# Output projections turned round (512 tokens move past stationary weights), the second norm's row factor moved into what follows it, and x reordered by loads

## The chip, the cores and the metric

One Trainium2 chip, one of its cores. Five engines work side by side, each through its own list of instructions in order: TensorE (PE; its weight loads are listed as PEld), VectorE (DVE), ScalarE (ACT), GpSimd (POOL), and SyncE (SP), which here issues all DMAs. The metric is the time of one execution in microseconds, as the median of several runs; lower is better.

## The reference

Two layers over 1024 tokens and 1024 model columns, all float32:

```python
def reference(x, positions, norm_g, fox_w_in, ..., dsw_w_out):
    cos, sin = rotary_tables(positions)
    for i in range(DEPTH):                      # DEPTH = 2
        h = rms_norm(x, norm_g[i])
        if i % N_MIXERS == 0:                   # layer 1: forgetting attention, 16 heads of 64, causal
            o, gate = fox_mixer(h, fox_w_in[j], fox_b_f[j], fox_q_norm[j], fox_k_norm[j])
            w_out = fox_w_out[j]
        else:                                   # layer 2: 3 groups of dilated windows, dilations 1, 4, 16
            o, gate = dsw_mixer(h, cos, sin, dsw_w_in[j], dsw_q_norm[j], dsw_k_norm[j])
            w_out = dsw_w_out[j]
        x = x + (o * jax.nn.silu(gate)) @ w_out
    return x

def rms_norm(x, g):
    y = x * lax.rsqrt(jnp.mean(x * x, axis=-1, keepdims=True) + EPS) * g
```

The part that matters here is the end of each layer: the mixer's output times the gate, called y below, goes through a 1024 x 1024 output projection and is added to x; between the layers the sum is normed by rows (tokens) and becomes the input of layer 2. Layer 2 norms its queries and keys per head of 64, so that a factor on a whole token's row cancels there but for EPS; values and gates carry it.

## The kernel before, in words

**Operands.** TensorE takes the left operand by columns: `xh[p, k, s]` holds row k*128+p of the transposed activations for token s, rounded to float32r, and `xl` what the rounding left. Weights are split the same way into `w.slabs[k][:, 0]` (high) and `[:, 1]` (low): ACT rounds a slab (L286), POOL or DVE subtracts (L288). A product is three matmuls: xh with high, xh with low, xl with high. `project` (L305) makes one tile of 128 tokens: for each of 8 k it loads 128 x 128 of xh or xl as the stationary operand and moves up to 384 weight columns past it. The result `pj` lies with tokens on partitions.

**Stages, in order.** (1) Gate columns of layer 1 in three parts of 384, 256 and 384 columns (`PARTS`), written to DRAM as `gs_d`. (2) Eight pairs of heads: project q, k, v of a pair for 8 token tiles, with the attention of these tiles spread among the projections (`fox_tile`: scores in PSUM tile `s`, DVE's min pass L659, ACT's exp L493, split into two halves `ph`, a DMA transpose into `ptt` L500, products with the values into `o`). Outputs y go to DRAM `y_d`; for the last pair they stay. (3) Output projection of layer 1, three parts by 8 token tiles. (4) Gates of layer 2. (5) 24 steps of dilated attention. (6) Output projection of layer 2.

**The order of the work.** PE's order is written out: `Flow` counts ticks (one for each two k of a projection, four for a token tile, 32 for a part), and work is queued for a tick (`flow.at`). `due` and `lsd` in `CFG` say at which ticks attention comes. The other engines and SP's list of DMAs are ordered by a list scheduler from that; each engine, and SP too, then runs its list strictly in order, so that a waiting instruction holds up those behind it.

**Turning y.** y has tokens on partitions and must be turned before a projection. `turn_y` loads seven of eight column blocks of a token tile back from `y_d` and turns them on PE (`transpose_rows`, L324), then ACT copies to xh (L327) and DVE makes xl (L328). The eighth block, of the last pair of heads, comes by `turn_last`. In stage 3, `project(..., t)` for a tile t needs the y of this tile alone.

**Between the layers.** In the third part of stage 3, each token tile's finished row of the sum, `xf`, is collected (two thirds of it loaded back from `x1_d`), normed on the spot (`norm_rows`: sums of squares on ACT, factor, product with the gain row `gbc` on DVE), written to `xn_d`, and turned by eight PE transposes into xh and xl for stage 4 (L785). In the eighth step of stage 5, `reload_x` (L917) loads the same rows from `xn_d` in another token order (every fourth token) and turns them on PE once more.

**Pools.** PSUM tiles: `pj` in a pool of three, scores `s` in three, `o` in two. x and sums for stage 3 pass through `n2k`, three buffers.

## Time and profile before

| what | value |
|---|---|
| time, median of 3 runs (lowest to highest) | 1817.96 us (1817.16 to 1822.23) |
| time of the profiled execution | 1825.77 us |
| its span, in which the trace lies | 1824.0 us |
| PE busy in the span | 1756.8 us (96%) |
| DVE, ACT, POOL busy | 1110.7, 985.2, 950.9 us |
| mean granted clock of TensorE | 0.992 |
| stage 3 (first to last of its additions) | 538.2 to 672.0 us |
| stage 4 (first to last of its gate inputs, L475) | 678.2 to 766.1 us |
| stage 6 (first to last of its additions) | 1727.9 to 1821.1 us |

The stages' ends are read from the first and last start of the lines L777, L780, L475 and L979. A group's row in the profile says how long instructions of a kind ran and how long their engine had stood idle before them; the timeline puts that idle time in brackets, with what ended it. A window's row says how much of a stretch each engine was busy; the rest of PE's stretch is its idle time.

### The profile page before, as it was taken

To read this page: it belongs to the slowest core of one execution; us is meant where nothing else is said; L and a number is where in the kernel's file an instruction comes from. 1 tells how busy PE (TensorE), PEld (TensorE's weight loads), DVE (VectorE), ACT (ScalarE), POOL (GpSimd) and SP (SyncE) were. 2 spreads that over 40 slices of the span, in tenths; PEclk is the share of its full clock that TensorE was granted. 3 is DMA by queue.
4 is the path that set the end of the run, shared out by engine and by line. 5 is a ranking of instruction groups with operands and counts; after the bars stand their busy time and mean duration, and the time that the engine had idled before them with its cause. 6 is when DMAs were issued, how large, how long until landed. Compare 5 with 4: busy or idle time off the path is not lost.

```text
span 1824.0 us, 39234 instructions
## 1 busy us (share of the span) xinstructions
PE 1756.8 (96%) x13784; PEld 1691.7 (93%) x13784; DVE 1110.7 (61%) x3774; ACT 985.2 (54%) x2642; POOL 950.9 (52%) x1161
## 2 busy tenths in 40 slices
PE   7999999999979989999999999999999999999999
PEld 6999888888868989999999999999999999999899
DVE  8546666766665373365556665676676766767631
ACT  6536666666664354445555565555555555555610
POOL 3215666556653211255556555667576666757520
PEclk9999999999999999999999999999999999999999
DMA  8347999899998563356676786676776766667852
GB/s 286 114 119 139 183 202 187 174 178 185 200 201 186 166 205 112 114 114 140 125 142 138 157 193 133 146 154 145 145 152 153 166 148 139 154 143 176 196 140 93
DMA packets 630790, 289.28 MB, mean 159 GB/s; under 512 B 510384, under 2 KB 595376, under 8 KB 630592
## 3 DMA queue, kind: packets, MB, share of 16 engines
q1 hardware_dynamic: 630592, 286.77, 69.1%
q8 instruction: 108, 1.77, 0.4%
q14 instruction: 90, 0.74, 0.1%
HBM read 124.87 MB, written 37.03 MB: 89 GB/s over the span
## 4 chain that ended last, share of the span: by engine, by line
PE 45%; DMA 21%; DVE 10%; ACT 8%; POOL 7%; issue 7%; SPq 1%; DVEq 0%; POOLq 0%; ACTq 0%
PE pj L312 40%; DMA raw<-in_w_dsw 6%; DMA ptt<-ph 4%; DMA raw<-in_w_fox 3%; POOL w L288 3%; PE s L448 2%; POOL ph L499 2%; DMA qk_t<-hl 2%; DVE p L659 2%; ACT p L493 2%; ACT ph L496 1%; POOL hl L423 1%; DMA raw<-in_w_fgate 1%; DMA x_d<-xo 1%; DVE u L420 1%
## 5 line engine op out<-in xcount | busy, mean ns | idle before, releaser
L312 PE MATMUL pj<-w,xh 128*128 128x384 f32 (+2 forms) x5632 | 1446.9, 340 | 23.8 <-ACT w L286 6.5
L312 PEld LDWEIGHTS pj<-w,xh 128*128 128x128 f32 x5632 | 1002.4, 191 | 33.7 <-ACT w L286 6.5
L312 PE MATMUL pj<-w,xl 128*128 128x384 f32 (+2 forms) x2816 | 941.7, 334 | 5.0 <-DVE xl L328 2.4
L312 PEld LDWEIGHTS pj<-w,xl 128*128 128x128 f32 x2816 | 537.3, 191 | 7.0 <-DVE xl L531 3.7
L288 POOL TENSOR_TENSOR w<-raw,w 128x384 fp32r<-128x384 f32 (+2 forms) x258 | 261.6, 1034 | 311.2 <-ACT w L286 271.5
L499 POOL TENSOR_TENSOR ph<-p,ph 128x512 f16<-128x512 f32 (+3 forms) x176 | 173.6, 1003 | 157.9 <-ACT ph L496 130.9
L286 ACT CAST w<-raw 128x384 fp32r<-128x384 f32 (+2 forms) x352 | 162.2, 501 | 124.7 <-PE pj L312 54.1
L423 POOL TENSOR_TENSOR hl<-u,hl 128x512 f16<-128x512 f32 x128 | 150.6, 1177 | 130.6 <-ACT hl L422 130.5
L850 POOL TENSOR_TENSOR ph<-p,ph 128x768 f16<-128x768 f32 (+2 forms) x96 | 155.7, 1622 | 106.0 <-ACT ph L849 103.6
L378 ACT ACTIVATE sq<-pj 128x256 f32<-128x256 f32 x256 | 96.8, 378 | 196.5 <-DVE u L373 194.8
L448 PE MATMUL s<-qk_t 128*128 128x128 f16 (+1 forms) x1504 | 160.3, 247 | 8.8 <-DVE acc L659 5.0
L255 DVE TENSOR_REDUCE vm<-raw 128x1 f32<-128x256 f32 x128 | 53.6, 419 | 152.9 <-DMA raw<-in_w_dsw 111.4
L507 PEld LDWEIGHTS <-ptt 128*128 128x128 f16 x1136 | 103.3, 98 | 41.9 <-issue 23.9
L448 PEld LDWEIGHTS <-qk_t 128*128 128x128 f16 x1504 | 110.2, 98 | 24.9 <-issue 14.2
L493 ACT ACTIVATE p<-p,acc 128x512 f32<-128x512 f32 (+2 forms) x192 | 109.9, 610 | 38.6 <-DVE acc L659 34.6
L422 ACT CAST hl<-u 128x512 f16<-128x512 f32 x128 | 79.1, 618 | 91.3 <-DVE u L420 86.1
L496 ACT CAST ph<-p 128x512 f16<-128x512 f32 (+3 forms) x176 | 89.2, 536 | 61.4 <-DMA ptt<-ph 61.3
L391 DVE TENSOR_REDUCE pj<-sq 128x8 f32<-128x512 f32 x128 | 88.4, 691 | 48.4 <-ACT sq L378 48.3
L845 ACT ACTIVATE p<-p,og 128x128 f32<-128x128 f32 (+1 forms) x256 | 97.7, 441 | 32.6 <-DVE og L844 32.5
L373 DVE TENSOR_TENSOR u<-pj,gr 128x256 f32<-128x256 f32 x256 | 106.4, 416 | 10.7 <-PE pj L312 10.4
L424 DVE COPY hl<-hl 128x512 f16<-128x512 f16 x128 | 62.1, 485 | 79.5 <-POOL hl L423 79.5
L508 PEld LDWEIGHTS <-ptt 128*128 128x128 f16 x1136 | 106.1, 97 | 0.8 <-issue 0.8
(167 smaller groups left out, 2291.8 us busy)
## 6 DMA issues: line engine op xcount, KB each, us to landing
raw<-in_w_dsw SPq DMA_DIRECT2D x96, 384.0 KB, 3.7
raw<-in_w_fox SPq DMA_DIRECT2D x32, 384.0 KB, 3.7
og_d<-og SPq DMA_DIRECT2D x64, 132.0 KB, 2.8
cmb<-og_d SPq DMA_DIRECT2D x64, 132.0 KB, 3.3
bc<-c_d SPq DMA_DIRECT2D x32, 256.0 KB, 4.1
gs_d<-ge SPq DMA_DIRECT2D x32, 192.0 KB, 2.3
xt<-in_xt SPq DMA_DIRECT2D x16, 256.0 KB, 6.1
xrow<-in_x SPq DMA_DIRECT2D x8, 512.0 KB, 7.0
```

Of the source, the lines that this page charges most:

```text
L286: nc.scalar.copy(w[:, 0, :n], raw[:, k % 2, :n])
L288: eng.tensor_sub(w[:, 1, :n], raw[:, k % 2, :n], w[:, 0, :n].bitcast(F32))
L312: nc.tensor.matmul(ps[:, :n], a[:, k, cols], w.slabs[k][:, j, :n], start=(k == 0 and i == 0), stop=(k == KT - 1 and i == 2))
L373: nc.vector.tensor_mul(u[:, t % 2].rearrange("p (a b) d -> p a b d", a=2), ps[:, : 4 * HD].rearrange("p (a b d) -> p a b d", a=2, b=2), gr ...
L423: nc.gpsimd.tensor_sub(hl[:, :, :4, 1], u, hl[:, :, :4, 0])
L448: nc.tensor.matmul(s[:, c0 : c0 + cnt * P].rearrange("p (c s) -> p c s", c=cnt), qk[:, i, blk], kk[:, j : j + cnt, e], start=(h == 0), sto ...
L493: nc.scalar.activation(p, p, AF.Exp, bias=acc, scale=-1.0)
L496: nc.scalar.copy(ph[:, e, 0, cols], p)
L499: (nc.gpsimd if pool_l else nc.vector).tensor_sub(ph[:, e, 1, cols], p, ph[:, e, 0, cols])
L507: nc.tensor.matmul(o[:, e, :], hi, vt[:, j, e, HD:], start=(b == 0), stop=False, skip_group_check=True)
L508: nc.tensor.matmul(o[:, e, :HD], hi, vt[:, j, e, :HD], start=False, stop=False, skip_group_check=True)
L850: nc.gpsimd.tensor_sub(ph[:, 1], st["p"], ph[:, 0])
```

## The change

- **`project_t`** takes the place of `project` in both output projections. The stationary operand is a 128 x 128 block of the weights, and 512 tokens of xh or xl move past it; the result has columns on partitions and tokens along the row. An output tile is (half b of the tokens, block m of 128 columns); there are 16. In the first part (three blocks m) the loops run k 0 to 3 of all three blocks, then k 4 to 6, then k 7, first for b = 0, then b = 1; in the other parts block by block.
- x for it comes from a new input `xp` laid out on the host; x1, xn and the output are stored by columns (`x1_d`, `xn_d` are [D, S]), the host turns the output back.
- **`grown`** follows each output tile of layer 1: DVE adds x (and puts tokens in the order of stage 5's second group), ACT multiplies with the gain (a number for each partition now), ACT squares, POOL adds up the squares.
- **`sums`, `factors`**: a matmul with ones adds the squares over partitions, the sums go through DRAM (`ss_d`) to tokens on partitions in the three token orders, and give `rx2`. Layer 2's gates and its values take the factor from `rx2` (`vsr`, one DVE instruction in each of the 24 steps), the head norms take EPS times it.
- **`take`, `reload_x`** load xn in the wanted order from `xn_d`, ACT and DVE split it into xh and xl. The 64 transposes of xn and the 64 of `reload_x` on PE are gone; those of y stay, now in the scores' PSUM pool and with high priority for their copies.
- The last pair of heads comes two ticks earlier, its qk transposes two ticks earlier, `turn_last` a tick later; `lsd` puts layer 2's last two steps later.

```diff
+    def project_t(h, w, done):
+        n = w.n // P
+        todo = []
+        for b in range(2):
+            ms = [[m] for m in range(n)] if h else [list(range(n))]
+            for mm in ms:
+                for ks in [range(KT)] if h else [range(4), range(4, KT - 1), range(KT - 1, KT)]:
+                    todo.extend((b, m, k) for m in mm for k in ks)
...
+            if k == 0:
+                ps[m] = ps_pj.tile([P, 512], F32, name="pj", tag="pj")
+            for x, (j, a) in enumerate(((0, xh), (0, xl), (1, xh))):
+                nc.tensor.matmul(ps[m], w.slabs[k][:, j, m * P : (m + 1) * P], a[:, k, 512 * b : 512 * (b + 1)], start=(k == 0 and x == 0), stop=(k == KT - 1 and x == 2))
+            if k == KT - 1:
+                done(b, PARTS[h][0] // P + m, ps[m])
...
-        pt = ps_o.tile([P, 512], F32, name="pt", tag="o") if own else ps_pj.tile([P, 512], F32, name="pt", tag="pj")
+        pt = ps_s.tile([P, 512], F32, name="pt", tag="s")
...
+        with tc.high_priority(cfg["ph_"]):
+            nc.scalar.copy(dh, pv)
+            nc.vector.tensor_sub(xl[:, k0 : k0 + n, t * P : (t + 1) * P], pv, dh.bitcast(F32))
...
+    def grown(b, m, ps):
+        xr = sb.tile([P, 512], F32, name="xr", tag="n2k", bufs=cfg["nb"])
+        nc.sync.dma_start(xr, ins["xp"][m, b])
+        xv = xr.rearrange("p (z s) -> p z s", z=4)
+        nc.vector.tensor_add(xv, ps.rearrange("p (s z) -> p z s", z=4), xv)
+        nc.sync.dma_start(halves(x1_d, m, b), xv)
+        xg = lay([P, 512], F32, name="xg", tag="p")
+        nc.scalar.activation(xg, xr, AF.Copy, scale=gt2[:, m : m + 1])
+        nc.sync.dma_start(halves(xn_d, m, b), xg.rearrange("p (z s) -> p z s", z=4))
+        if m == 0:
+            nc.scalar.activation(acc[:, b], xr, AF.Square)
+        else:
+            sq = lay([P, 512], F32, name="nsq", tag="p")
+            nc.scalar.activation(sq, xr, AF.Square)
+            nc.gpsimd.tensor_add(acc[:, b], acc[:, b], sq)
+    def sums(b):
+        so = ps_o.tile([P, 512], F32, name="so", tag="o")
+        nc.tensor.matmul(so[:1], ones[:, :1].bitcast(F32), acc[:, b], start=True, stop=True)
...
+        nc.sync.dma_start(ss_d.rearrange("(b o s) -> b o s", b=2, o=1)[b], row[:1])
+        ssq = lay([P, 3 * NT], F32, name="ssq", tag="gsl")
+        g0 = ss_d.rearrange("(b t p) -> b p t", b=2, p=P)[b]
+        nc.sync.dma_start(ssq[:, 4 * b : 4 * b + 4], g0)
+        if b == 0:
+            return factors(ssq, 0, 4)
+        for z in range(4):
+            nc.sync.dma_start(ssq[:, 8 + 2 * z : 10 + 2 * z], ss_d.rearrange("(b p z) -> z p b", b=2, z=4)[z])
+        nc.sync.dma_start(ssq[:, 16:], ss_d.rearrange("(p t) -> p t", t=NT))
+        factors(ssq, 4, 3 * NT)
+    def take(b, m):
+        xs = lay([P, 512], F32, name="xs", tag="ga")
+        nc.sync.dma_start(xs.rearrange("p (z s) -> p z s", z=4), halves(xn_d, m, b))
...
+            nc.scalar.copy(dh, xv)
+            nc.vector.tensor_sub(dl, xv, dh.bitcast(F32))
...
-            if h == 2:
-                xf = rows2("xf")
-                nc.sync.dma_start(xf[0], x1_d[rows, :512])
...
-                xn = norm_rows(xf, gbc2)
-                for i in range(2):
-                    nc.sync.dma_start(xn_d[rows, i * 512 : (i + 1) * 512], xn[i])
-                    flow.at(flow.now + cfg["lx"] + i, lambda xn=xn, i=i, t=t: transpose_half(xn[i], i, t))
+        if h == 2:
+            for b, (a, d) in enumerate(((11, 2), (28, 1))):
+                for m in range(KT):
+                    def get(b=b, m=m, s1=s0 + (17, 33)[b] + m * d):
+                        flow.at(s1, take(b, m))
+                    flow.at(s0 + max(a + m * d, (0, 0, 0, 0, 0, 6, 12, 17)[m] + 16 * b), get)
+                flow.at(s0 + 16 * (b + 1) + 8, lambda b=b: sums(b))
+        project_t(h, w, grown)
...
-            flow.at(flow.now + 5 + h, lambda h=h: transpose_half(xt[h], h, t, True))
+            xt = lay([P, 4, P], F32, name="x2", tag="ga")
+            nc.sync.dma_start(xt, xn_d.rearrange("(h k p) c -> h p k c", k=4, p=P)[h, :, :, t * P : (t + 1) * P])
...
+        vsr = sm.tile([P, NT], F32, name="vsr", tag="vsr")
+        nc.vector.tensor_scalar(vsr, rx2[:, 0, g * NT : (g + 1) * NT], w.vs, None, ALU.mult)
...
+        project_t(h, w, finished)
...
-  lsd=((16, 16), (14, 11), (12, 10))
+  lsd=((16, 16), (16, 14), (14, 11))
```

**PE in the first part of layer 1's output projection, behind the scores of the last token tile's second head.** L448 and L450 are score products, L657 and L656 the causal mask added to them; L324 and L346 transpose y (`yt`: blocks loaded back, `y`: the last pair's block); L312 is a product of `project`, L336 one of `project_t`; o<-vt,ptt are products with the values. First before, then after:

```order
L448 MATMUL s<-qk_t 128x256
L657 LDWEIGHTS ident_b
L657 MATMUL s<-tri_b,ident_b 128x128
L324 MATMUL pt<-ident,yt 128x128 x3
L324 MATMUL pt<-ident,y 128x128
L312 MATMUL pj<-w,xh 128x384 x2
```

```order
L656 LDWEIGHTS ident_b
L656 MATMUL s<-tri_b,ident_b 128x128
L336 MATMUL pj<-xh,w 128x512
L336 MATMUL pj<-xl,w 128x512
L336 MATMUL pj<-xh,w 128x512 x2
L336 MATMUL pj<-xl,w 128x512
L336 MATMUL pj<-xh,w 128x512
L346 MATMUL pt<-ident,yt 128x128 x3
L346 MATMUL pt<-ident,y 128x128
```

In both, two turns of y follow the scores. Before, their PSUM tiles are in the pools of `o` and `pj`; now they are the next two tiles of the scores' own pool of three, and of the six products ahead of them three end the first half's sums and three begin the second half's.

**SP at the same place**, where the last attention of layer 1 still runs. L500 and L499 are the DMA transposes of the last tiles' probabilities, L778 and L780 the stores of the sum, L783 the stores of xn, L819 the loads of `take`, L769 and L777 the loads of x, L357 and L363 the gain row. First before, then after:

```order
L778 DMA x_d<-xo 128x384
L500 DMA_TRANSPOSE ptt<-ph 128x14x128
L769 DMA xr<-in_x 128x384
L500 DMA_TRANSPOSE ptt<-ph 128x16x128
L778 DMA x_d<-xo 128x384
L500 DMA_TRANSPOSE ptt<-ph 128x16x128
L769 DMA xr<-in_x 128x384
L357 DMA gbc<-in_norm_g 128x1024
```

```order
L783 DMA xn_d<-xg 512x1x128
L780 DMA x_d<-xr 512x1x128
L777 DMA xr<-in_xp 128x512
L819 DMA xs<-xn_d 128x4x128
L777 DMA xr<-in_xp 128x512
L819 DMA xs<-xn_d 128x4x128
L499 DMA_TRANSPOSE ptt<-ph 128x16x128
L783 DMA xn_d<-xg 512x1x128
L777 DMA xr<-in_xp 128x512
L363 DMA gbc<-in_norm_g 128x1024
L499 DMA_TRANSPOSE ptt<-ph 128x16x128
```

The last two transposes stood between single stores and loads of x. They now stand behind stores of the first half's sums and behind loads that read these stores back, and the very last one behind the gain row, whose buffer comes from the pool of `ph`.

152 lines of the change are left out of this document (74 added, 78 removed).

## Prediction

> **What bounds the kernel now.** I read the page's engine table first, then windows by stage, then PE's timeline for its gaps. From the page:
>
> ```profile
> span 1824.0 us, 39234 instructions
> PE 1756.8 (96%) x13784; PEld 1691.7 (93%) x13784; DVE 1110.7 (61%) x3774; ACT 985.2 (54%) x2642; POOL 950.9 (52%) x1161
> ```
>
> PE is the bound; only work taken off it, or gaps closed in it, count. The windows say where gaps are (us of the stretch, busy time and count by engine, granted clock, DMA share, GB/s):
>
> ```profile
> 500.00:530.00 30.00, 26.79 (x287) 23.89 (x284) 21.62 (x69) 20.61 (x48) 16.35 (x15) 1.00 1.02 197
> 530.00:595.00 65.00, 56.03 (x541) 51.06 (x539) 35.06 (x117) 29.99 (x68) 23.32 (x25) 0.92 0.83 189
> 595.00:640.00 45.00, 41.87 (x299) 41.11 (x299) 13.34 (x39) 14.32 (x35) 11.60 (x12) 1.00 0.59 175
> 640.00:680.00 40.00, 35.42 (x198) 33.24 (x197) 29.11 (x70) 20.24 (x57) 6.38 (x6) 0.91 0.64 214
> 680.00:766.00 86.00, 85.54 (x553) 85.17 (x553) 32.62 (x71) 41.78 (x91) 14.27 (x16) 1.00 0.33 100
> 1045.00:1100.00 55.00, 54.24 (x433) 52.76 (x431) 37.66 (x122) 36.72 (x95) 31.54 (x38) 1.00 0.83 191
> 1100.00:1680.00 580.00, 573.97 (x4305) 558.87 (x4304) 390.73 (x1465) 318.28 (x951) 385.45 (x530) 1.00 0.68 151
> 1680.00:1745.00 65.00, 60.45 (x459) 56.28 (x458) 40.25 (x136) 37.29 (x106) 36.08 (x48) 1.00 0.79 184
> ```
>
> From 500 to 595 (the last pair of heads and the first part of layer 1's projection) PE stands idle 3.2 + 9.0 = 12.2 us, from 595 to 680 (its other parts) 3.1 + 4.6 = 7.7, from 1680 to 1745 (layer 2's tail) 4.55, while 580 us of dilated attention hold only 6.0. So the change works where PE's gaps are. The largest gaps, with what ended them, and two rows after the last:
>
> ```profile
> 544.59 1.12 PE L324 MATMUL pt<-ident,yt 128*128 128x128 f32 x4 [4.04 <-DVE xl L328]
> 590.94 0.44 PE L312 MATMUL pj<-w,xl 128*128 128x384 f32 x1 [2.45 <-DVE xl L328]
> 623.47 0.59 PE L312 MATMUL pj<-w,xh 128*128 128x384 f32 x2 [2.35 <-DVE xo L777]
> 646.97 1.01 PE L312 MATMUL pj<-w,xh 128*128 128x384 f32 x2 [3.73 <-DVE xl L328]
> 648.10 0.84 PE L312 MATMUL pj<-w,xh 128*128 128x384 f32 x2
> 649.06 0.84 PE L312 MATMUL pj<-w,xh 128*128 128x384 f32 x2
> ```
>
> Two belong to turning y, one to an addition that waited for x, one to the turning of xn. After the last, three products take 0.96 us; the pace below is 0.53. The granted clock of 0.92 over 65 us and 0.91 over 40 is such slow spells: 5.2 + 3.6 = 8.8 us of clock missing. Part of it falls into the idle time, so I count 6.8 as lost: 4.2 before 595, 2.6 after. Idle and slow together: 16.4 us and 10.3 us.
>
> **Matmuls, wider.** PE's starts in pure projections, for rows of 384, 256 and 272 columns:
>
> ```profile
> 699.88 0.51 PE L312 MATMUL pj<-w,xh 128*128 128x384 f32 x2
> 700.41 0.52 PE L312 MATMUL pj<-w,xh 128*128 128x384 f32 x2
> 708.33 0.40 PE L312 MATMUL pj<-w,xh 128*128 128x256 f32 x2
> 708.68 0.40 PE L312 MATMUL pj<-w,xh 128*128 128x256 f32 x2
> 63.24 0.42 PE L312 MATMUL pj<-w,xh 128*128 128x272 f32 x2
> 63.62 0.42 PE L312 MATMUL pj<-w,xh 128*128 128x272 f32 x2
> ```
>
> Three products take 0.53, 0.355 and 0.38 us: 0.1767, 0.118 and 0.127 each, a line of 0.45 ns a column and a few ns. At 512 it gives 0.234; in proportion to 384 it is 0.236. A projection was 384 of 384 columns and 192 of 256, 67.8 + 22.8 = 90.6 us, and becomes 384 of 512, 89.9 to 90.5. Two projections: -1.3, at worst -0.2.
>
> The Trainium skill, page "TensorE: Matmul & The Clock Gate", section "Back-to-back issue gap", gives N/2.4 + 2.5 ns for a lone stream. By it 512 columns take 0.2158 us and a projection 82.9, an estimate of -15 for both. It would make 384 columns 0.1625, which the rows above contradict.
>
> **Transposes of x.** They go; groups of four, and one of them in its surroundings:
>
> ```profile
> L324 PE MATMUL pt<-ident,x 128*128 128x128 f32 x64 | 9.6, 272 | 0.0
> L324 PE MATMUL pt<-ident,xn 128*128 128x128 f32 x64 | 10.2, 283 | 1.2 <-DVE xl L328 0.7 <-DVE xf L780 0.5
> 1048.95 0.60 PE L324 MATMUL pt<-ident,x 128*128 128x128 f32 x4
> 1049.30 0.60 PE L312 MATMUL pj<-w,xh 128*128 128x384 f32 x2
> 1049.92 0.52 PE L312 MATMUL pj<-w,xh 128*128 128x384 f32 x2
> ```
>
> Four transposes hold PE 0.35 us, and the next three products take 0.62 instead of 0.53: 0.44 a group. 128 transposes are 32 groups: -14.1. PE was full there, so this is path. The 0.76 us idle in 1045 to 1100 was a wait for such a copy: -0.8. ACT's and DVE's copies stay in number and size, reading loads instead of PSUM.
>
> **Layer 1's projection, parts two and three.** The wait for x, the collected rows, and the turned xn are gone; 10.3 us hung on them. What comes instead: each output tile is 24 x 0.234 = 5.6 us of PE. Its buffer of x needs a load, an addition and a store; the nearest rows:
>
> ```profile
> xr<-in_x SPq DMA_DIRECT2D x16, 192.0 KB, 3.5
> xn_d<-xn SPq DMA_DIRECT2D x16, 256.0 KB, 2.9
> x<-xn_d SPq DMA_DIRECT2D x16, 256.0 KB, 3.7
> L979 DVE TENSOR_TENSOR xr<-pj,xr 128x384 f32<-128x384 f32 x16 | 8.9, 557 | 35.9 <-PE pj L312 35.7
> L345 ACT ACTIVATE nsq<-xf 128x512 f32<-128x512 f32 x16 | 10.1, 630 | 22.1 <-DMA xf<-x_d 14.4 <-DVE xf L780 7.7
> L327 ACT CAST xh<-pt 128x512 fp32r<-128x512 f32 x48 | 27.7, 579 | 10.5 <-PE pt L324 10.4
> L328 DVE TENSOR_TENSOR xl<-pt,xh 128x512 fp32r<-128x512 f32 x48 | 33.0, 687 | 18.5 <-ACT xh L327 18.0
> ```
>
> Load 3.5, addition 0.557 x 512/384 = 0.74, two ACT passes 1.3, store 2.9: 8.4 us against three buffers x 5.6 = 16.8. ACT and DVE have under 2.8 us of work in 5.6. At the seam, the last tile needs 0.74 + 0.63 + 2.9 + 3.7 + 0.58 + 0.69 = 9.2 us from its last product to xl, and its tokens are read only by the fifth token tile of the gates, 4 x 24 x 0.1767 = 17 us on; with that cover gone it would cost its excess. I leave 1.0 us: -9.3.
>
> **The last pair of heads and part one.** Two new waits stand in the order. Behind the last scores, the second of two turns of y takes the scores' third buffer, which DVE frees by its pass over them; ahead of that pass DVE has the third addition of the half (0.74) and the xl of the first turn, which waits for ACT. From the half's last product: 0.74, about 1.3 for ACT and xl, 0.7 for the pass is 2.7, less three products and the turn (1.0): 2 us or more, with its slow spell 3 to 4. Second, SP:
>
> ```profile
> ptt<-ph SPq DMA_TRANSPOSE x18, 4.5
> gbc<-in_norm_g SPq DMA_DIRECT2D x1, 512.0 KB, 4.6
> ```
>
> The last DMA transpose sits behind the gain row, which waits for a buffer of `ph`, so for the transpose before it: store of xn 2.9 and its reload's turn, 4.5, then 4.5 again, some 13 us from the half's end. Cover until its products: 42 x 0.234 = 9.8 plus 3 of values, 13 us: 0 to 3 us. DVE then waits for the gain row (4.6 us, then its maximum) ahead of the last y: 1 to 2, as at 590.94 now. Earlier loads of y and priority for its copies take away the rest, 4.04 above all. I keep 8 of 16.4: -8.4 (bounds -15 and +4).
>
> The slow spells are what speaks against bundling waits. The same page, section "What's actually happening", says an idle window of about 3.4 us halves the clock, the window running freely. Here 2.45 us did it and 2.35 did not; by the rule taken strictly the new 2-us waits would cost no spell, some 2 us less than I count.
>
> **Layer 2's tail.** Half-wise reading lets four token tiles' last y come before k = 7, and 36 products of cover precede k = 4. Of 4.55 idle I keep 3: -1.5 (bounds -4.5 and +3). The last addition grows 0.2, the last store by a third: +0.7.
>
> **What is added.** Two matmuls with ones over 512 float32 columns: four transposes' columns, 0.35 each, up to four products, 0.94: +0.7. `vsr`:
>
> ```profile
> L739 DVE TENSOR_SCALAR vsr<-rx,vs 128x8 f32<-128x8 f32 x8 | 8.4, 1048 | 0.0
> bfb<-in_b_f SPq DMA_DIRECT2D x1, 8.0 KB, 7.9
> ```
>
> 24 x 1.05 = 25 us on DVE, which is 67% busy from 1100 to 1680 while PE's three `pj` buffers carry 12 us; if that cover failed all 25 would show. I take +1.0. The gates' longer inputs, the layer's EPS and POOL's 14 sums cost nothing: in 680 to 766 DVE, ACT and POOL are under half busy, and POOL in part two and three a quarter.
>
> **The sum.** -1.3 - 14.1 - 0.8 - 9.3 - 8.4 - 1.5 + 0.7 + 0.7 + 1.0 = -33.0. The profiled execution took 1825.8 us, 1.8 outside its span, and becomes 1792.8. It stands 7.8 above the median of 1818.0; on the median's footing the forecast is 1785.
>
> **Rivals.** (a) The gaps come back elsewhere: turning y in the scores' pool and SP's longer list give part one its 16.4 again, and the seam its 10.3. Then -33 + 8.4 + 9.3 + 1.5 = -14, 1804. For it: DMA share is 0.83 to 1.02 there, and everything passes one SP list. Against: both large gaps had causes that are gone. (b) All gaps close: -8.0 - 3.0 - 1.0 more, 1773. (c) The wide products run at the page's pace: 0.2158 instead of 0.234, 768 x 0.018 = 14 less, 1771; three widths on one line speak against. (d) Slower: the factor for the second half of the tokens and for the other orders comes by five loads of 4- and 32-byte runs behind a store. The gates' fifth tile needs it 17 us on and PE can run three tiles further, 13 us; 8.5 us pass before the sums' matmul, and some 4 go to it, ACT and the store, so about 17 are left. If loads took 7.9 each as the 8-KB one above and ran one after another, 39.5 in all, PE would lose 22; from 10 each, 50 in all, the gain of 33 is gone. At 12 PE loses 60 - 17 = 43, and the time is 1785 + 43 = 1828. That row fell in the crowded first microseconds, so little speaks for it. (e) The change does its work but DVE shows all of `vsr`: +24, 1809.
>
> **Chances.** Forecast (1778 to 1796) 0.55; (a) with (e) 0.22; (b) and (c) 0.14; (d) 0.05; something between that leaves no change 0.04. The range 1770 to 1809 leaves out (d) and no change. About 0.3%, 5.5 us, is what a measurement tells from no change: faster 0.91, same 0.04, slower 0.05.
>
> **What would show it.** Right: no transposes of x; starts of 512-column products 0.234 apart; gaps from the half's end of part one to its last k, none over 1 us in parts two and three; stage 4 unchanged at 88 us. Wrong: a granted clock under 0.9 in part one, PE waiting for `ge` in the gates, or DVE's `u` ending PE's waits in the 24 steps.

## The result, and the profile after

The changed kernel takes 1831.1 us (median of 4 runs, 1829.0 to 1831.7) against 1818.5 for the kernel before (4 runs, 1817.2 to 1822.2). The ratio is 1.0064, 95% interval 1.0047 to 1.0081: slower by 12 us, where the prediction said 33 faster. From the page of the changed kernel:

```profile
span 1829.6 us, 38158 instructions
PE 1746.2 (95%) x13276; PEld 1647.2 (90%) x13276; DVE 1115.0 (61%) x3738; ACT 999.6 (55%) x2632; POOL 974.0 (53%) x1175
```

PE has 508 matmuls less and is 10.6 us less busy, but the span grew by 5.6: PE's idle time grew. The same windows as before, of the changed kernel:

```profile
500.00:530.00 30.00, 26.36 (x260) 23.89 (x260) 17.84 (x60) 17.41 (x41) 14.10 (x14) 0.94 0.89 179
530.00:595.00 65.00, 54.89 (x527) 43.85 (x523) 34.22 (x108) 37.88 (x85) 32.46 (x33) 0.93 1.00 211
595.00:640.00 45.00, 44.06 (x186) 35.64 (x184) 19.92 (x41) 19.43 (x35) 19.46 (x17) 0.95 0.67 205
640.00:680.00 40.00, 35.73 (x156) 28.81 (x155) 23.24 (x29) 25.65 (x40) 13.93 (x11) 0.96 0.64 185
1045.00:1100.00 55.00, 50.96 (x398) 49.25 (x397) 41.06 (x113) 35.72 (x91) 33.68 (x36) 0.97 0.84 187
1100.00:1680.00 580.00, 564.50 (x4188) 548.67 (x4187) 388.20 (x1456) 314.61 (x941) 380.94 (x523) 1.00 0.68 148
```

From 500 to 680 PE is idle 3.6 + 10.1 + 0.9 + 4.3 = 18.9 us where it was 19.9, and the clock that is missing comes to 1.8 + 4.6 + 2.3 + 1.6 = 10.3 us where it was 8.8. From 1045 to 1100 it is idle 4.0 instead of 0.8, from 1100 to 1680 15.5 instead of 6.0.

The profile of before that the prediction used is of an execution 7 us slower than the runs' median, so the comparison goes on with a second one of the same kernel (run b2 below, 1818.6 us). For the way through the program I count the 256 starts of DVE's `u<-pj,gr` (one for each token tile of a pair of heads): number 57 opens the last pair of heads, number 65 layer 2's first step of 24, 113 the seventh, 129 the ninth, 249 the last.

| stretch, us | before (b2) | changed | measured difference | forecast |
|---|---|---|---|---|
| start to the last pair of heads | 476.5 | 480.6 | +4.1 | 0 |
| last pair, projection, seam, gates of layer 2 | 291.1 | 284.5 | -6.6 | -24.7 |
| steps 1 to 6 | 237.5 | 242.1 | +4.6 | +0.25 |
| steps 7 and 8 (reload_x) | 86.7 | 87.1 | +0.4 | -7.75 |
| steps 9 to 23 | 584.9 | 594.3 | +9.4 | +0.6 |
| step 24 to the last addition | 136.6 | 137.2 | +0.6 | -1.4 |
| sum | 1813.3 | 1825.8 | +12.5 | -33 |

The forecast column is the prediction's sum cut at these places. Against the first profile of before the differences are +1.6, -7.5, +2.2, -0.2, +7.9 and +1.2, so single rows carry an uncertainty of some 2 us. The first row is mostly luck of single executions: up to there both kernels do the same work but for a few loads and their order, and the two profiles of before differ by 4.9 us at its start and 2.5 at its end. Over all profiles below the stretch took 476.5 to 479.0 us in before and its variants and 476.8 to 484.2 in the variants of the changed kernel; whether a part of it belongs to the change is not shown. In the second row 6.6 us came, about the work taken off PE there (0.65 + 7.05 - 0.7 = 7.0); the waits that were to close did not. The rest has four questions: the steps, the eighth step, the seam (between layer 1's projection and the gates of layer 2), and part one of layer 1's projection.

### The profile page after: what moved, and what is told of

Read it like the earlier page. It is cut to its first block, busy times and chain, and to the rows that moved or that the text cites. A ratio compares the mean times of both kernels' runs of the same rounds, so it can differ in the third digit from the quotient of the medians.

```text
span 1829.6 us, 38158 instructions
## 1 busy us (share of the span) xinstructions
PE 1746.2 (95%) x13276; PEld 1647.2 (90%) x13276; DVE 1115.0 (61%) x3738; ACT 999.6 (55%) x2632; POOL 974.0 (53%) x1175
## 4 chain that ended last, share of the span: by engine, by line
PE 48%; DMA 20%; DVE 12%; ACT 7%; POOL 6%; issue 5%; SPq 1%; POOLq 0%; DVEq 0%; ACTq 0%
PE pj L313 37%; PE pj L336 6%; DMA raw<-in_w_dsw 6%; DMA ptt<-ph 5%; PE s L450 3%; DMA qk_t<-hl 3%; POOL w L291 2%; POOL ph L498 2%; DVE p L658 2%; ACT p L492 2%; DMA raw<-in_w_fox 2%; ACT ph L495 2%; DVE w L291 1%; POOL hl L425 1%; DMA og_d<-og 1%
## 5 line engine op out<-in xcount | busy, mean ns | idle before, releaser
L313 PE MATMUL pj<-w,xh 128*128 128x384 f32 (+2 forms) x4864 | 1261.9, 341 | 31.7 <-DVE u L422 8.2
L313 PEld LDWEIGHTS pj<-w,xh 128*128 128x128 f32 x4864 | 874.1, 192 | 43.0 <-ACT vt L388 9.9
L313 PE MATMUL pj<-w,xl 128*128 128x384 f32 (+2 forms) x2432 | 817.6, 336 | 2.7 <-DVE xl L530 2.7
L313 PEld LDWEIGHTS pj<-w,xl 128*128 128x128 f32 x2432 | 464.9, 191 | 3.4 <-DVE xl L530 3.4
L291 POOL TENSOR_TENSOR w<-raw,w 128x384 fp32r<-128x384 f32 (+2 forms) x258 | 260.2, 1027 | 239.9 <-ACT w L289 236.8
L910 POOL TENSOR_TENSOR ph<-p,ph 128x768 f16<-128x768 f32 (+2 forms) x96 | 155.2, 1617 | 106.7 <-ACT ph L909 106.7
L450 PE MATMUL s<-qk_t 128*128 128x128 f16 (+1 forms) x1504 | 163.6, 250 | 15.7 <-DMA qk_t<-hl 7.1
L336 PE MATMUL pj<-xh,w 128*128 128x512 f32 x512 | 171.3, 406 | 2.1 <-ACT p L905 1.1
L506 PEld LDWEIGHTS <-ptt 128*128 128x128 f16 x1136 | 104.2, 99 | 51.1 <-issue 28.6
L450 PEld LDWEIGHTS <-qk_t 128*128 128x128 f16 x1504 | 111.6, 99 | 33.7 <-issue 12.6
L389 DVE SCALAR_TENSOR_TENSOR vt<-pj,vsr,vt 128x128 f16<-128x128 f32 x256 | 89.5, 350 | 84.9 <-ACT vt L388 84.3
L336 PEld LDWEIGHTS pj<-xh,w 128*128 128x128 f32 x512 | 98.5, 192 | 24.4 <-DVE xr L779 1.4
```

The lines of the kernel that those rows point to most:

```text
L291: eng.tensor_sub(w[:, 1, :n], raw[:, k % 2, :n], w[:, 0, :n].bitcast(F32))
L313: nc.tensor.matmul(ps[:, :n], a[:, k, cols], w.slabs[k][:, j, :n], start=(k == 0 and i == 0), stop=(k == KT - 1 and i == 2))
L336: nc.tensor.matmul(ps[m], w.slabs[k][:, j, m * P : (m + 1) * P], a[:, k, 512 * b : 512 * (b + 1)], start=(k == 0 and x == 0), stop=(k == K ...
L450: nc.tensor.matmul(s[:, c0 : c0 + cnt * P].rearrange("p (c s) -> p c s", c=cnt), qk[:, i, blk], kk[:, j : j + cnt, e], start=(h == 0), sto ...
L506: nc.tensor.matmul(o[:, e, :], hi, vt[:, j, e, HD:], start=(b == 0), stop=False, skip_group_check=True)
L910: nc.gpsimd.tensor_sub(ph[:, 1], st["p"], ph[:, 0])
```

## The experiments

Ratios are to the kernel before on the same chip, with 95% intervals. V is the changed kernel with `vsr` on ACT, D is V with the first factors taken without DRAM. Names that begin with b_ change the kernel before, a_ the changed kernel, v_ V, d_ D.

| kernel | ratio to before | interval |
|---|---|---|
| changed kernel | 1.0064 | 1.0047 to 1.0081 |
| before + `vsr` on DVE (b_vsr) | 1.0078 | 1.0047 to 1.0108 |
| V (a_vsr_act) | 1.0028 | 1.0014 to 1.0041 |
| changed, y turned in the pool of `o` (a_turn_o) | 1.0119 | 1.0089 to 1.0148 |
| V, gain row later (v_gbc) | 1.0037 | 1.0022 to 1.0051 |
| V, seven buffers for reload_x (v_reload) | 1.0020 | 1.0003 to 1.0036 |
| D (v_direct) | 0.9988 | 0.9975 to 1.0001 |
| D with the edits of v_gbc and v_reload (v_all) | 0.9999 | 0.9983 to 1.0015 |
| D, y rounded on DVE (d_turn_dve) | 1.0005 | 0.9989 to 1.0020 |
| D, xl of reload_x on POOL (d_pool_xl) | 1.0056 | 1.0034 to 1.0078 |
| D, reload_x without xl (d_noxl) | 0.9994 | 0.9980 to 1.0008 |
| D without reload_x (d_noreload) | 0.9970 | 0.9958 to 0.9982 |
| before without reload_x (b_noreload) | 0.9950 | 0.9935 to 0.9966 |
| d_noreload without the norm in part one (d_nonorm) | 0.9937 | 0.9921 to 0.9953 |
| D, the first sum later (d_late) | 1.0005 | 0.9991 to 1.0018 |
| D, the norm in part one later (d_defer) | 0.9982 | 0.9968 to 0.9995 |
| D, both (d_best) | 0.9986 | 0.9973 to 1.0000 |
| d_defer, gain row at the start (d_early) | 0.9964 | 0.9952 to 0.9977 |

**Noise first (b2).**

> The kernel before once more, for a second profile of it. Its profiled execution took 1825.8 us where the median of its runs is 1818, and its first 500 us and those of the changed kernel hold the same instructions but for the names of two loads. Theory: those 7 us are the luck of that one execution (waits for the DMA transposes of the probabilities), so this one ends near 1818 and its eight pairs of heads differ by 2 to 5 us from the first profile. Rival: they belong to the program, and the second profile shows the same stage times within 1 us and a total near 1825.

1818.6 us, one run. The profiles differ by 4.9 us already where the heads begin and by 7.2 us at the end, in no one place: luck. From these two profiles, a profile alone cannot place differences below some 4 us; below, a wait is named from profiles, its price from the runs.

**The steps: `vsr`.** Undone (V) and added alone to the kernel before (b_vsr):

```diff
-        nc.vector.tensor_scalar(vsr, rx2[:, 0, g * NT : (g + 1) * NT], w.vs, None, ALU.mult)
+        nc.scalar.activation(vsr, rx2[:, 0, g * NT : (g + 1) * NT], AF.Copy, scale=w.vs)
```

> The changed kernel with one edit: the 24 products of layer 2's row factor and the value scale (`vsr`, 128x8) run on ACT instead of DVE. In the profile of the changed kernel 14 of the 24 took 0.98 to 1.06 us on DVE, each as long as an add that POOL ran at that moment, and 9 took 0.22 where POOL's last add had just ended; the milestones of the 24 steps slip by 12 us between step 8 and step 21. Theory A (vsr on DVE holds up the step's chain of u): 7 to 12 us less than the changed kernel, 1819 to 1824, and the waits of 0.9 to 1.4 us for DVE's u in every second step go. Rival B (the steps are late for another cause: loads, the DMA transposes qk_t, the new place of the last two steps): under 3 us, 1828 or more, and the waits for u stay.

```diff
+    one8 = const.tile([P, NT], F32, name="one8")
+    nc.vector.memset(one8, 1.0)
...
+        vsr = sm.tile([P, NT], F32, name="vsr", tag="vsr")
+        nc.vector.tensor_scalar(vsr, one8, w.vs, None, ALU.mult)
...
-            heads_tile(ps, g + 1, t, hd, vt, w.vs)
+            heads_tile(ps, g + 1, t, hd, vt, vsr[:, t : t + 1])
```

> The kernel before with one addition: in each of the 24 steps of layer 2 the value scale goes through a DVE product of 128x8 as in the changed kernel, here with ones in the place of the row factor, so that the numbers stay the same. Theory A (that product holds up the step): 7 to 12 us more than before, 1825 to 1830. Rival B (DVE has the room for it, as the prediction counted): 0 to 2 us more.

Both answers speak for theory A, though neither lies in its 7 to 12 us: V stands 0.36% (6.5 us) below the changed kernel, and 24 such products added alone cost 0.78%, 14 us (8.5 to 19.6). The window from 1100 to 1680 us of before (b2), of b_vsr and of V, in this order:

```profile
1100.00:1680.00 580.00, 573.85 (x4298) 558.74 (x4297) 385.42 (x1465) 319.83 (x958) 387.68 (x530) 1.00 0.69 151
```
```profile
1100.00:1680.00 580.00, 565.58 (x4240) 549.57 (x4239) 393.41 (x1471) 317.28 (x948) 381.30 (x525) 1.00 0.69 148
```
```profile
1100.00:1680.00 580.00, 572.41 (x4255) 558.46 (x4254) 388.98 (x1463) 321.67 (x971) 386.69 (x533) 1.00 0.70 152
```

PE idles 6.2, 14.4 and 7.6 us; the changed kernel 15.5. Of that, waits for DVE's `u` are 1.8, 8.7 and 5.2 us, 8.2 in the changed kernel: added with the product, they went only in part with it. DVE is 66 to 68% busy in these windows. What makes 1.05 us of an instruction on 1024 numbers stands beside it in the timeline of the changed kernel; DVE and POOL, first where it is long, then where it is short:

```profile
1326.08 1.05 DVE L994 TENSOR_SCALAR vsr<-rx,vs 128x8 f32<-128x8 f32 x1
1326.09 2.10 POOL L291 TENSOR_TENSOR w<-raw,w 128x384 fp32r<-128x384 f32 x2
...
1364.89 1.05 POOL L291 TENSOR_TENSOR w<-raw,w 128x384 fp32r<-128x384 f32 x1
1365.01 0.99 DVE L462 TENSOR_SCALAR vt<-vs 128x16 f16<-128x16 f32 x1
1365.89 0.22 DVE L994 TENSOR_SCALAR vsr<-rx,vs 128x8 f32<-128x8 f32 x1
```

(L291, like L910 below, is a subtraction; the expectations call such instructions POOL's adds.) Where POOL's instruction is just ending and no other follows, `vsr` takes 0.22; where the next one starts with it, it ends with that one. Of the 24, 15 took 0.98 to 1.06, one 0.50 and 8 took 0.22 (the expectation has 14 and 9). It stands ahead of the copy of `hl` and of `u`, for which PE's scores and its next projection wait: what counts is not DVE's load but a delay in the one chain whose slack is short, as the waits for `u` show. The Trainium skill, page "SBUF — State Buffer", section "Who interferes with whom", says that a tensor_scalar of DVE in a two-port mode and an instruction of POOL exclude each other for a whole instruction. The rows agree with the exclusion (1.05 against 0.22 us); in which mode DVE ran they do not show.

**The seam: the factors.** In V, PE waits for the gates' weights in three places, as in the changed kernel, whose rows are (PE; DVE; ACT):

```profile
666.71 0.44 PE L313 MATMUL pj<-w,xh 128*128 128x384 f32 x1 [0.65 <-ACT w L289]
668.61 0.45 PE L313 MATMUL pj<-w,xh 128*128 128x384 f32 x1 [1.46 <-DVE w L291]
670.49 0.45 PE L313 MATMUL pj<-w,xh 128*128 128x384 f32 x1 [1.09 <-POOL w L291]
```
```profile
665.84 0.17 DVE L811 TENSOR_SCALAR sv<-ssq 128x4 f32<-128x4 f32 x1 [5.86 <-DMA ssq<-ss_d]
```
```profile
666.04 0.21 ACT L355 ACTIVATE rx<-sv 128x4 f32<-128x4 f32 x1 [3.55 <-DVE sv L811]
666.16 0.50 ACT L289 CAST w<-raw 128x384 fp32r<-128x384 f32 x1
```

DVE stands 5.86 us before four sums that come back from DRAM, ACT behind it, and ACT's casts of the weights behind that. The products that wait here need weights and not these sums: what waits for the sums is the list. D takes them from PSUM:

```diff
+        if b == 0:
+            s4 = ps_o.tile([P, 512], F32, name="s4", tag="o")
+            for t in range(4):
+                nc.tensor.matmul(s4[:, t : t + 1], nat[0][:, P * t : P * t + P], ones[:, :1].bitcast(F32), start=True, stop=True)
+            factors(s4, 0, 4)
...
```

> The changed kernel with the 24 products on ACT (called V below), and a second edit: the first half's sums of squares are also taken by four small products that leave tokens on partitions in PSUM, so that the first half's factors need no store to DRAM and no load back (the other sums still go that way). In V's profile DVE waits 5.9 us for that load behind the last tiles of part three, ACT behind it, and behind ACT's factor stand two casts of the gates' weights: PE waits 0.46, 1.45 and 1.08 us for these weights. Theory A (the factor's way through DRAM holds up the weights): these three waits go, 2 to 4 us less than V, which measured 1.0028 of before. Rival B (the weights' own loads and casts are late): the waits stay within 1 us in sum.

The three waits are gone and D is 0.40% (7 us) below V, more than the 3 us of the waits. The runs show that the edit helps; the profiles do not show where: from the last pair to layer 2's steps V took 281.3 us and D 281.2. V's profile is of its quickest run, 4 us below its median. In D's list PE now waits longer for POOL's last sum of squares, 2.56 us where V waits 0.90:

```profile
649.65 0.59 PE L801 MATMUL so<-snat,ones 128*1 128x512 f32 x1 [2.56 <-POOL snat L794]
```

d_late moves that product four ticks down (`+ 8` becomes `+ 12` for b = 0).

> D with one more edit: the product with ones over the first half's squares stands four ticks later in PE's list (D's first factors need no trip through DRAM, so they can wait). In D PE waits 2.6 us for POOL's last sum of squares at that place (0.9 to 1.1 in the changed kernel and V). Theory A (that wait is a plain loss): it goes, 2 to 3 us less than D. Rival B (PE then waits as long for the gates' weights or for the first gates' factor): 0 to 1 us less.

No gain (0.17% above D, the intervals overlap): the wait went to the other half's sum (2.39 us at 671.95) and to a weight (1.23), much as rival B said.

**The eighth step.** First more buffers:

```diff
+            if h:
+                xt = sb.tile([P, 4, P], F32, name="x2b", tag="n2k", bufs=cfg["nb"])
...
```

> V with a second edit: every second load of reload_x goes to a buffer of the pool of sums (three, idle there), so that the loads have seven buffers instead of four. In V's profile the eighth step has no transposes of x and yet takes as long as before (86.7 and 87.1 us from step 7 to step 9): an x load on SP waits 8 us for a buffer that DVE's xl frees (before, PE's transposes freed it), the weight loads behind it come late, DVE's maximum over them waits 4.1 us, and PE waits 2.49 us for vt and 2.69 for qk_t, with a slow spell. Theory A (the buffers of x): those waits go, 4 to 7 us less than V, and the step reaches the 7.8 us that the prediction gave it. Rival B (DVE's xl from SBUF, 0.7 to 2.1 us each where it shares time with POOL's adds against 0.69 from PSUM, is too much for the step): under 2 us less, and PE still waits for vt.

Within the intervals of V, and PE still waits 2.15 us for vt and 2.39 for qk_t: the theory of the buffers fell. The rows of V (POOL; DVE; PE) show the other one:

```profile
1040.02 2.15 POOL L910 TENSOR_TENSOR ph<-p,ph 128x1024 f16<-128x1024 f32 x1
```
```profile
1040.61 2.11 DVE L986 TENSOR_TENSOR xl<-x,xh 128x512 fp32r<-128x512 f32 x1
1042.64 0.41 DVE L378 TENSOR_TENSOR u<-pj,gr 128x256 f32<-128x256 f32 x1
1042.98 1.15 DVE L986 TENSOR_TENSOR xl<-x,xh 128x512 fp32r<-128x512 f32 x1
...
1044.12 0.34 DVE L389 SCALAR_TENSOR_TENSOR vt<-pj,vsr,vt 128x128 f16<-128x128 f32 x1
```
```profile
1044.52 0.44 PE L313 MATMUL pj<-w,xh 128*128 128x384 f32 x1 [2.49 <-DVE vt L389]
1056.69 0.28 PE L450 MATMUL s<-qk_t 128*128 128x128 f16 x2 [2.69 <-DMA qk_t<-hl]
```

DVE's xl ends only after POOL's subtraction, with `u` and `vt` behind it. Is the step set by PE at all? Leave reload_x out, in before and in D; leave only xl out; give xl to POOL. (Without reload_x the last 16 steps work on x in its first order, without its xl on a remainder in that order; these kernels show a price and are no versions.)

```diff
-                reload_x(t)
+                pass
```

> The kernel before without reload_x: the 64 transposes of x in the eighth step, their loads and their copies on ACT and DVE are left out, so the last 16 steps work on x in its first order. It shows the most that taking these transposes off PE can bring. Theory A (PE sets the pace of that step, as the prediction had it): the step from 1005 to 1092 us falls from 86.7 to about 79, the whole by 7 to 8 us. Rival B (the heads' chain over DVE, ACT, POOL and SP sets it nearly as much, and the transposes were work that PE did while it would have waited): the step falls by less than 4, with new waits of PE for u, vt or qk_t.

> D without reload_x: loads, rounding and subtraction of x in the eighth step are left out (the last 16 steps work on x in its first order). In the kernel before, taking reload_x out brought 7.0 us in that step and 0.5% in all. Theory A (the step costs D as much as it cost before, only elsewhere: through DVE and SP instead of PE): the step (step 7 to step 9) falls from 85.5 to about 79.5, 5 to 8 us less than D. Rival B (the step is bound by something else that the change brought): the step stays above 84.

```diff
-                nc.vector.tensor_sub(xl[:, 4 * h : 4 * h + 4, t * P : (t + 1) * P], xt, dh.bitcast(F32))
```

> D with reload_x but without its 16 subtractions on DVE (xl keeps its first order; the loads and the rounding to xh on ACT stay). Theory A (DVE's subtractions, held by POOL's adds, are what costs the step its gain): the step falls to within 1.5 us of D without reload_x, and PE's waits for vt (1.9 us) and qk_t (2.3 us) go. Rival B (the loads in SP's list cost it: weight loads and DMA transposes stand behind them): the step stays within 2 us of D's 85.5, with the wait for qk_t.

```diff
-                nc.vector.tensor_sub(xl[...], xt, dh.bitcast(F32))
+                nc.gpsimd.tensor_sub(xl[...], xt, dh.bitcast(F32))
```

> D with one more edit: the 16 subtractions that make xl in reload_x run on POOL instead of DVE. In V and its variants the first of them took 2.1 to 2.6 us on DVE while an add of POOL ran, and u and vt stood behind it; PE waited 1.9 to 2.5 us for vt. Theory A (DVE's subtraction with both inputs in SBUF is held by POOL's adds): PE's wait for vt falls below 0.7 us, 1 to 3 us less than D. Rival B (the step is bound by the heads' chain in any case): PE waits as long for u or qk_t, 0 to 2 us more, since POOL has 16 subtractions of some 1.2 us more in that chain.

Steps 7 and 8 take 86.7 us in before and 79.7 without reload_x: PE did set the pace, and the forecast of 7.0 for the transposes was right as a price, the copies included that went with them (whole kernel: 9 us, 6 to 12). In D they take 85.5, without xl 82.8, without reload_x 80.4. So loads and splits cost D 5.1 of the 7.0, about half of it by xl; d_noxl lies between its theory and its rival. Without xl, PE's wait for vt is 0.48 instead of 1.88, that for qk_t stays:

```profile
1059.45 0.23 PE L450 MATMUL s<-qk_t 128*128 128x128 f16 x1 [1.74 <-DMA qk_t<-hl]
```

With xl on POOL the wait for vt is 0.53, as theory A said, but POOL's part of the heads comes late, and with it qk_t; the kernel is 0.68% (12 us) above D, far more than the 2 us of rival B:

```profile
1062.78 0.40 PE L450 MATMUL s<-qk_t 128*128 128x128 f16 x2 [9.84 <-DMA qk_t<-hl]
```

In the runs the differences are smaller than in the profiles (D to d_noxl +0.06%, D to d_noreload -0.18%, the intervals overlap); the split between xl and loads rests on one profile each.

**Part one.** The prediction let 8 of 16.4 us stand here; none of the rest was saved (from 500 to 595 us PE idles 13.7 us where it was 12.2). PE's waits in the changed kernel, and ACT and DVE ahead of the first:

```profile
541.49 0.28 PE L450 MATMUL s<-qk_t 128*128 128x128 f16 x2 [2.72 <-DVE xl L351]
...
575.39 0.33 PE L346 MATMUL pt<-ident,y 128*128 128x128 f32 x1 [2.43 <-DVE xl L351]
...
593.68 0.24 PE L506 MATMUL o<-vt,ptt 128*128 128x65 f16 x1 [3.73 <-DMA ptt<-ph]
```
```profile
539.33 1.14 ACT L495 CAST ph<-p 128x512 f16<-128x512 f32 x2 [1.68 <-DMA ptt<-ph]
540.37 0.64 ACT L350 CAST xh<-pt 128x384 fp32r<-128x384 f32 x2
```
```profile
540.88 0.56 DVE L351 TENSOR_TENSOR xl<-pt,xh 128x384 fp32r<-128x384 f32 x1 [1.91 <-ACT xh L350]
```

A scores product waits for a PSUM tile that holds a turned y; ACT rounds that y only behind casts of `ph` that wait for a DMA transpose. So attention waits for y and y for attention. The edits: y in another pool, the gain row later, y rounded on another engine, the norm out of part one or later in it, the gain row at the start.

```diff
-        pt = ps_s.tile([P, 512], F32, name="pt", tag="s")
+        pt = ps_o.tile([P, 512], F32, name="pt", tag="o")
```

> The changed kernel with one edit: the PSUM tile in which y is turned comes from the pool of `o` (two buffers) instead of the scores' pool (three). In the first part of layer 1's projection PE waited 2.72, 0.92 and 2.43 us for the xl of a turned y, twice with scores behind it. Theory A (the scores' pool is the cause): these waits go, with their spells at half clock, 5 to 8 us less, 1823 to 1826. Rival B (the turning itself is late, because ACT's copy stands behind the casts of ph): the wait moves to the products with the values, which now stand behind the turned y, and the time stays within 3 us of the changed kernel.

Worse by 0.55% (10 us), which neither theory allowed: with two buffers for y and `o`, PE waits for xl in seven places instead of three, up to 3.49 us (at 529.73). The scores' pool was the better of the two.

```diff
-            load_gbc(1)
+            flow.at(s0 + 8, lambda: load_gbc(1))
```

> V with a second edit: the gain row of layer 2 (512 KB) is loaded eight ticks later, so that on SP it stands behind the last DMA transpose of layer 1 and not ahead of it. In V's profile PE waits 2.98 us for that transpose, with a slow spell behind it. Theory A (the gain row holds the transpose up): the wait shrinks below 1 us, 2 to 4 us less than V. Rival B (the transpose is late by its own chain, from the scores over ACT and POOL, and by the stores ahead of it): the wait stays above 2 us, 0 to 1 us less.

The wait for the last transpose is 1.94 us where V has 2.98, and one of 3.15 for an xl came, which stands on DVE behind the maximum over the gain row (2.69 us of waiting for it): no gain, but by another way than rival B said.

> V with the three edits together: factors of the first half without DRAM, seven buffers for reload_x, the gain row behind the last transpose. If each does what its theory A says, 8 to 14 us less than V, 0.995 to 0.998 of before; if none does, V's 1.003.

v_all is no better than D, as its two other parts weren't better than V.

```diff
-            nc.scalar.copy(dh, pv)
+            nc.vector.tensor_copy(dh, pv)
```

> V with the factors of the first half without DRAM (called D below; it measured 0.9988 of before), and one more edit: the rounding of turned y to xh runs on DVE instead of ACT, ahead of its xl on the same engine. In the first part of layer 1's projection PE waits 2.3 and 1.4 us for xl of a turned y in D (2.7 and 2.4 in the changed kernel), where ACT's cast of y stands behind casts of ph that wait for a DMA transpose. Theory A (ACT's list is what holds up the turned y): the two waits shrink below 1 us each, 2 to 5 us less than D. Rival B (DVE is as late as ACT there, with up to 0.7 us more for each turn): the waits stay or move, the time is within 2 us of D or above it.

The waits for xl, 2.29 and 1.40 us in D, are 0.81 and 1.33, but a wait for qk_t (2.83 us at 542.89) and one of 4.16 for the last transpose came: 0.17% above D, inside the noise.

d_nonorm, which also leaves reload_x out, returns from `grown` behind the store of x1 for the blocks m < 3 and does not read them back, so the gates lack these blocks; d_defer queues that share six ticks later:

```diff
+        flow.at(flow.now + (6 if m < 3 else 0), norm)
```

> D without reload_x, and without the norm's share of the first part of layer 1's projection: for its three blocks of columns the product with the gain, the squares, the store of xn and the reading back are left out (six blocks of sixteen; their x1 is still stored). To be compared with D without reload_x. Theory A (in part one the stores of xn, the loads of `take` and ACT's passes stand ahead of the last turns of y and of the last DMA transposes): PE's waits of 1.4 us for xl and of 1.8 and 1.7 us for the transposes go, part one ends 4 to 7 us earlier, while the wait of 2.3 us at 540 us, which comes ahead of the first sum, stays. Rival B (these waits come from the attention's own chain and the turned y in the scores' pool): they stay within 1.5 us in sum, and the kernel gains under 2 us there.

> D with one more edit: in the first part of layer 1's projection the norm's share of a finished block (gain, squares, store of xn) is queued six ticks later, so that it stands behind the last turn of y of the first half on ACT, and its stores behind more of the DMA transposes on SP. Leaving this share out altogether brought 6 us (0.33%), and PE's waits of 1.4 to 2.2 us for xl and 1.7 to 2.9 for the last transpose were gone, with a new one of 3.1 us for an xl behind the gain row. Theory A (the share costs by where it stands): 2 to 5 us less than D. Rival B (it costs by its amount, wherever it stands in part one or two): under 1 us less.

> D with both edits, the later product and the later share of the norm. If both theories A hold, 4 to 8 us less than D, 0.994 to 0.997 of before; if neither does, D's 0.999.

Without the norm's share the kernel is 0.33% (6 us) quicker than d_noreload: these 3 x 2 passes of gain and squares, their stores, the loads of `take` and their splits are a real part of the bill. The waits at 574 and 592 are gone, one of 1.89 us for a transpose stays and one of 3.12 us for xl is new. Put later, they cost hardly less: d_defer is 0.06% below D, inside the noise, and with the later sum (d_best, 0.9986) nothing is added. In the place of the later waits for xl and for the last transpose stands one for y itself,

```profile
595.80 0.48 PE L346 MATMUL pt<-ident,y 128*128 128x128 f32 x1 [4.20 <-DVE y L691]
```

and ahead of that y on DVE stands the maximum over the gain row:

```profile
593.87 1.22 DVE L365 TENSOR_REDUCE gmax<-gbc 128x1 f32<-128x1024 f32 x1 [3.24 <-DMA gbc<-in_norm_g]
```

The same row had stood ahead of the xl in v_gbc. d_early takes it and its maximum at the start of the kernel, behind those of layer 1:

```diff
-            load_gbc(1)
+            flow.at(48, lambda: load_gbc(1))
```

> d_defer with one more edit: the gain row of layer 2 and its maximum are taken at the start, right behind those of layer 1, and no longer in the first part of layer 1's projection. In d_defer DVE waits there 3.2 us for that row and takes 1.2 for its maximum, ahead of the last y, and PE then waits 4.2 us for that y. Theory A (the gain row is what stands ahead of the last y): that wait falls below 1.5 us, 2 to 4 us less than d_defer, 0.996 to 0.997 of before. Rival B (another wait of the attention's chain takes its place, or the row costs as much among the first loads): within 1 us of d_defer.

```profile
530.00:595.00 65.00, 57.41 (x547) 46.47 (x547) 38.50 (x128) 39.46 (x88) 34.45 (x35) 0.95 1.02 207
595.00:640.00 45.00, 45.00 (x198) 36.86 (x197) 14.20 (x28) 22.14 (x39) 20.55 (x18) 1.00 0.75 229
```

The wait for y is 2.93 us and not under 1.5, but the windows hold 57.4 and 45.0 us of PE, where d_defer had 55.6 and 44.2, and the stretch from the last pair to layer 2's steps is 279.1 us (before 291.1, changed 284.5). d_early is 0.18% below d_defer (the intervals overlap), 0.24% below D and 0.36% (6.5 us) faster than before: the version that beats both kernels. The gain row taken early without the later norm was not run. My reading of part one: three lists (ACT's casts, DVE's gain row, SP's transposes) end there within a few us of one another, so that an edit to one opens a wait on another, and PE gains only after the second or third is out of the way. That fits the waits named above; no run shows it by itself. PE's waits for the first turn of y (2.91 us at 544.17) stay open: d_turn_dve shrank the one there, and a wait for qk_t came in its place.

## Why the prediction was wrong, point by point

- **Matmuls, wider: right, and too small.** Starts of the 512-column products in the last projection of the changed kernel:

```profile
1790.35 0.62 PE L336 MATMUL pj<-xh,w 128*128 128x512 f32 x2
1790.81 0.39 PE L336 MATMUL pj<-xl,w 128*128 128x512 f32 x1
1791.04 0.62 PE L336 MATMUL pj<-xh,w 128*128 128x512 f32 x2
```

  Three take 0.69 us, 0.229 each; 384 of them are 88.0 us against 90.6, so -5.2 for two projections and not -1.3. The pace is between the line through 384 and 256 columns (0.234) and 0.2158, which rival (c) took.
- **Transposes of x, -14.1: the price right, the cover wrong.** Its sentence "ACT's and DVE's copies stay in number and size, reading loads instead of PSUM" is the step that failed. In number they stay; the xl of 512 columns takes 0.689 us in the mean from PSUM and 1.006 (reload_x) and 1.140 (`take`) from a load:

```profile
L351 DVE TENSOR_TENSOR xl<-pt,xh 128x512 fp32r<-128x512 f32 x16 | 11.0, 689 | 6.4 <-ACT xh L350 6.4
L986 DVE TENSOR_TENSOR xl<-x,xh 128x512 fp32r<-128x512 f32 x16 | 16.1, 1006 | 2.1 <-ACT xh L985 1.9
L825 DVE TENSOR_TENSOR xl<-xs,xh 128x512 fp32r<-128x512 f32 x16 | 17.6, 1140 | 10.0 <-ACT xh L824 10.0
```

  The source alone is not what makes them longer: of reload_x's 16, ten took 0.68 or 0.69 as from PSUM, and six, which POOL's instructions overlapped, 0.85 to 2.27. Those of `take` took 1.08 to 1.12 also in the 11 cases without POOL beside them; they write every fourth element, but no run tests that as the cause. The wait for a copy in 1045 to 1100 (-0.8) did not go: PE waits there 2.5 us for `vt`, behind such a copy. The transposes of xn are gone from PE too, and about their price came in their stretch.
- **`vsr`, +1.0: mis-sized.** Its duration was taken high (25 us in all, 17.6 measured); the cover was not there. It costs 6.5 us by undoing it and 14 by adding it. The reason given, 67% of DVE and three buffers, is an average over steps, and the chain through `hl` and `u` has less slack than the buffers: the sign that the prediction itself had named, DVE's `u` ending PE's waits in the steps, came. Rival (e) named it, with 24 us as its price.
- **Last pair and part one, -8.4; seam, -9.3: neither came.** Both waits named for part one were there (the second turn of y 2.43 us, the last transpose 3.73), and a third, 2.72, of a scores product for the xl of a turned y, which was not named. The sum for the first (2.7 less 1.0) gives 1.7 and not the 2 or more that stands there, and an xl ended the wait where the prediction had the pass over the scores. The half-clock spells that it counted behind such waits came: the granted clock was 0.50 from 542 to 545 us, behind 2.72, and from 576 to 579, behind 2.43. So the step that failed is the size of what stays: 8 of 16.4 us in part one and 1.0 of 10.3 at the seam, with the old gaps closed and new ones as large in their place. Rival (a), "gaps return elsewhere", is what happened, from 500 to 680 us to within 1 us. At the seam the prediction looked for the factor's arrival (rival (d), for the second half of the tokens); it was the first half's factor, and it harmed not who needed it but who stood behind it. That a wait on DVE and ACT holds up the weights of the next stage was not asked. Even d_early takes 279.1 us from the last pair to layer 2's steps, where 291.1 - 24.7 = 266.4 was forecast; no run places the other 12.7.
- **Tail, -1.5 and +0.7:** the stretch took 0.6 us more although the wider products gave it 2.6, so its other terms came to +3.2 where -0.75 was forecast. Waits of 2.5 us (at 1725.13, ahead of a turn of y, its cause not in the trace) and 1.1 (at 1739.34) stand there. No experiment went to it, and the two profiles of before differ by 0.6 in it.
- The range, 1770 to 1809, took (a) and (e) one at a time, with 0.22 between them; added, 1804 + 24 = 1828 would have been near the measured time. They came together with the reload, and the three are alike: each time work or a wait went to the lists of DVE, ACT and SP, which were mostly counted by how busy they were.

## What to carry to other kernels

An engine that is 60 to 70% busy need not be cover for an instruction ahead of the one that the bound engine waits for: find that chain, and price each added instruction on it in full. Count an operation anew when its operands or their order in memory change, and look what another engine does beside it. And of a value that returns through memory, ask first who stands behind its reader in the same list.

## What the runs showed of the hardware that was not expected

A DVE product on 128x8 numbers took 0.22 us where POOL was done and up to 1.06 beside a subtraction of POOL; a subtraction of DVE on 128x512 with both inputs in SBUF took 0.68 alone and up to 2.57 (v_reload) where POOL's was already running, and 1.08 to 1.12 alone where it writes every fourth element (`take`). PE's idle times of 2.43 and 2.72 us were followed by half clock, one of 2.35 (before, at 623) was not. A TensorE product of 512 columns took 0.229 us, so that the step from 384 to 512 columns costs 0.41 ns a column, less than from 256 to 384 (0.46).
